# Attention probabilities of a two-layer encoder, transposed by VectorE in 32x32 blocks instead of by TensorE, with the heads in a written order

## The chip, the cores and the metric

The kernel runs on one core of a Trainium2 chip. The metric is the device time of one execution in microseconds. Five engines work beside each other, each through its own queue of instructions: TensorE (PE in the profile; its weight loads are PEld), VectorE (DVE), ScalarE (ACT), GpSimd (POOL) and SyncE (SP), which here issues DMAs.

## The reference, cut to what matters

Two layers; x is 512 x 1024 in float32. In each layer one projection feeds three kinds of attention with heads of 64 features, whose outputs are gated, merged and projected; then comes an MLP.

```python
h = x @ w_in[layer]
qa, ka, va, qb, kb, vb, qc, kc, vc, gate_logits = split(h)
oa = dilated_attention(rot(qa)*scale, rot(ka), va)                 # a: 4 heads, all 512 keys, masked
ob = softmax(axial(rms(qb))*scale @ axial(rms(kb)).T) @ vb         # b: 8 heads, 2 for keys and values
oc = neighbourhood_attention(qc*scale, kc, vc, rpb)                # c: 4 heads, 16-column windows, bias
g = sigmoid(gate_logits + b_gate)
merged = g0*(oa @ w_ba) + g1*(ob @ w_bb) + g2*(oc @ w_bc)
x = LN(alpha*x + merged @ w_out)
x = LN(alpha*x + square(relu(x @ w_up)) @ w_down)
```

## The kernel before, in words

Each float32 factor is held as a pair, hi (rounded) and lo (the rest), and `mm3` (lines 152 to 155) forms a product from three TensorE matmuls: hi hi, hi lo, lo hi. A unit of work below is one such `mm3`.

**Weights** come through `Stream`: SyncE issues a DMA of 512 KB into one of two `raw` buffers, ScalarE copies it to `whi` (line 182), VectorE subtracts to get `wlo` (line 183). A tile holds 8 units of work. Up to 5 split tiles are held, 3 more in a second pool after the heads.

**A layer** projects q and k of a (`a_qk`) and v of a, then goes through 64 blocks: 16 of a, 16 of c, 32 of b. A block is one head times 128 queries. It has two score matmuls (lines 513 and 514; 512 keys in a and b, 256 or 384 in c), the row maximum (line 519 for b, 523 with mask or bias for a and c), its negation (524), the exponential with its row sum (525, ScalarE), the reciprocal of the sum (528), the product with it (529; GpSimd, for c VectorE), and `turn`: TensorE transposes each 128x128 piece into PSUM (line 544, `psp`), and `split_psum` turns that into the pair `pth` (ScalarE, line 228) and `ptl` (VectorE, line 229). After the fourth block of a head, `values` multiplies with v in 8 matmuls; the output is evicted in lines 568 and 569, and for each second head split into `oh` and `ol`.

**Beside the blocks** two lists are served. `Work` holds the other matmuls of the layer (gates, the projections for b and c, the branch products with their results in `psg`, `psq`, `psb`); `pump(rate)` issues so many units twice per block. `Chores` holds small steps: `make_pair` and `prepare` transpose the queries and keys of a pair of heads and split them (lines 446 to 457), `norm_rotate` (lines 368 to 397) normalizes and rotates 128 rows of q and k of b, with a power on GpSimd (380) and sine products on GpSimd (389) between steps on VectorE. `need` (called when a new head begins) finishes whatever its q and k still lack.

**The order** of the instructions on each engine is set by a scheduler, except in the first projection, where the program order is kept. After the heads comes `tail` (gates and branch products of b, merged by line 617 on GpSimd), then the product with `w_out`, LN, the two halves of the MLP, and LN again. All of PSUM's 8 banks are one pool.

## Time and profile before

| | |
|---|---|
| median of 3 runs | 1546.57 us (1546.35 to 1548.46) |
| profiled execution | 1549.4 us, its span 1547.6 us |
| mean granted clock of TensorE | 0.996 |
| heads of layer 1 (46.3 to 302.7 us) | 256.4 us |
| heads of layer 2 (811.6 to 1068.7 us) | 257.1 us |

The span runs from the first to the last recorded instruction; the metric is a little longer. A busy time is the time in which an engine works on at least one instruction; matmuls overlap, so the mean duration of one is longer than the distance between two. Clock 1.00 is 2.4 GHz and 0.50 is 1.2 GHz.

### The profile page before, as it was taken

To read this page: it belongs to the slowest core of one execution; us is meant where nothing else is said; L and a number is where in the kernel's file an instruction comes from. 1 tells how busy PE (TensorE), PEld (TensorE's weight loads), DVE (VectorE), ACT (ScalarE), POOL (GpSimd) and SP (SyncE) were. 2 spreads that over 40 slices of the span, in tenths; PEclk is the share of its full clock that TensorE was granted. 3 is DMA by queue.
4 is the path that set the end of the run, shared out by engine and by line. 5 is a ranking of instruction groups with operands and counts; after the bars stand their busy time and mean duration, and the time that the engine had idled before them with its cause. 6 is when DMAs were issued, how large, how long until landed. Compare 5 with 4: busy or idle time off the path is not lost.

```text
span 1547.6 us, 19148 instructions
## 1 busy us (share of the span) xinstructions
PE 1527.6 (99%) x7400; PEld 1279.8 (83%) x7400; DVE 866.0 (56%) x1498; ACT 632.5 (41%) x1036; POOL 182.0 (12%) x190
## 2 busy tenths in 40 slices
PE   8999999999999999999999999999999999999997
PEld 6888888888898888888888888888888888888886
DVE  4678877644664314441566787776448542244315
ACT  4665666533144212431136556665332431134310
POOL 0113213211100000000102141233111000000001
PEclk9999999999999999999999999999999999999999
DMA  6222311153153323332331323112432432233311
GB/s 218 83 85 75 111 55 58 52 177 123 55 177 96 96 82 96 110 96 83 106 128 56 98 82 103 55 59 95 146 123 83 136 99 92 82 123 95 96 55 55
DMA packets 43434, 150.61 MB, mean 97 GB/s; under 512 B 5072, under 2 KB 5712, under 8 KB 43344
## 3 DMA queue, kind: packets, MB, share of 16 engines
q1 hardware_dynamic: 43344, 149.40, 30.5%
q8 instruction: 58, 0.95, 0.2%
q14 instruction: 32, 0.26, 0.1%
HBM read 145.19 MB, written 4.19 MB: 97 GB/s over the span
## 4 chain that ended last, share of the span: by engine, by line
PE 95%; DVE 2%; ACT 1%; DMA 1%; issue 0%; POOL 0%; SPq 0%; POOLq 0%; DVEq 0%; ACTq 0%
PE psd L155 9%; PE psd L154 9%; PE psd L153 9%; PE psu L154 8%; PE psu L155 8%; PE psu L153 8%; PE psg L155 6%; PE psg L154 6%; PE psg L153 6%; PE psp L544 3%; PE psq L155 2%; PE psq L153 2%; PE psq L154 2%; PE psb L155 2%; PE psb L153 2%; PE psb L154 2%
## 5 line engine op out<-in xcount | busy, mean ns | idle before, releaser
L183 DVE TENSOR_TENSOR wlo<-raw,whi 128x1024 fp32r<-128x1024 f32 (+1 forms) x246 | 306.9, 1248 | 421.5 <-ACT whi L182 420.5
L182 ACT ACTIVATE whi<-raw 128x1024 fp32r<-128x1024 f32 (+1 forms) x246 | 258.4, 1053 | 462.8 <-PE psd L155 143.1
L153 PE MATMUL psu<-xTh,whi 128*128 128x512 f32 (+1 forms) x576 | 210.8, 366 | 0.0
L154 PE MATMUL psu<-xTl,whi 128*128 128x512 f32 (+1 forms) x576 | 210.7, 366 | 0.0
L155 PE MATMUL psu<-xTh,wlo 128*128 128x512 f32 (+1 forms) x576 | 210.5, 365 | 0.0
L153 PE MATMUL psd<-whi,hh 128*128 128x512 f32 x512 | 199.3, 389 | 0.0
L155 PE MATMUL psd<-whi,hl 128*128 128x512 f32 x512 | 199.2, 389 | 0.0
L154 PE MATMUL psd<-wlo,hh 128*128 128x512 f32 x512 | 199.2, 389 | 0.0
L153 PE MATMUL psg<-xTh,whi 128*128 128x512 f32 x384 | 156.8, 408 | 0.0
L154 PE MATMUL psg<-xTl,whi 128*128 128x512 f32 x384 | 151.6, 395 | 0.0
L155 PE MATMUL psg<-xTh,wlo 128*128 128x512 f32 x384 | 151.6, 395 | 0.0
L154 PEld LDWEIGHTS psu<-xTl,whi 128*128 128x128 f32 x576 | 108.6, 189 | 17.7
L153 PEld LDWEIGHTS psu<-xTh,whi 128*128 128x128 f32 x576 | 108.6, 189 | 17.4
L155 PEld LDWEIGHTS psu<-xTh,wlo 128*128 128x128 f32 x576 | 108.6, 189 | 17.4
L266 POOL TENSOR_TENSOR ve<-ve,nhalf 128x1 f32<-128x1 f32 x16 | 24.2, 1513 | 775.0 <-DVE ve L265 775.0
L529 POOL TENSOR_SCALAR p<-p,stat 128x512 f32<-128x512 f32 x96 | 70.7, 737 | 360.2 <-DVE stat L528 242.9
L154 PEld LDWEIGHTS psd<-wlo,hh 128*128 128x128 f32 x512 | 96.1, 188 | 20.0
L153 PEld LDWEIGHTS psd<-whi,hh 128*128 128x128 f32 x512 | 96.1, 188 | 19.9
L155 PEld LDWEIGHTS psd<-whi,hl 128*128 128x128 f32 x512 | 96.1, 188 | 19.8
L153 PE MATMUL psq<-whi,xTh 128*128 128x512 f32 (+1 forms) x256 | 90.0, 351 | 7.2 <-ACT whi L182 6.7
L229 DVE TENSOR_TENSOR ptl<-psp,pth 128x512 fp32r<-128x512 f32 (+2 forms) x128 | 81.6, 637 | 21.2 <-ACT pth L228 19.8
L155 PE MATMUL psq<-whi,xTl 128*128 128x512 f32 (+1 forms) x256 | 87.9, 343 | 0.0
(116 smaller groups left out, 2572.7 us busy)
## 6 DMA issues: line engine op xcount, KB each, us to landing
raw<-in_w_up SPq DMA_DIRECT2D x64, 512.0 KB, 3.6
raw<-in_w_down SPq DMA_DIRECT2D x64, 512.0 KB, 3.5
raw<-in_w_gate SPq DMA_DIRECT2D x48, 512.0 KB, 3.5
raw<-in_w_qkv SPq DMA_DIRECT2D x22, 512.0 KB, 3.6
raw<-in_w_out SPq DMA_DIRECT2D x16, 512.0 KB, 3.6
raw<-in_w_c SPq DMA_DIRECT2D x12, 512.0 KB, 3.5
bias<-in_rpb SPq DMA_DIRECT2D x8, 640.0 KB, 3.9
raw<-in_w_bb SPq DMA_DIRECT2D x8, 512.0 KB, 3.6
```

Of the source, the lines that this page charges most:

```text
L153: nc.tensor.matmul(ps, lhs.hi, rhs.hi, start=start, stop=False)
L154: nc.tensor.matmul(ps, lhs.hi, rhs.lo, start=False, stop=False)
L155: nc.tensor.matmul(ps, lhs.lo, rhs.hi, start=False, stop=stop)
L182: nc.scalar.activation(hi[:, s], raw[:, s], AF.Copy)
L183: nc.vector.tensor_tensor(lo[:, s], raw[:, s], f32(hi[:, s]), op=ALU.subtract)
L229: nc.vector.tensor_tensor(dst.lo, ps, f32(dst.hi), op=ALU.subtract)
L266: nc.gpsimd.tensor_tensor(ve[:, 1:], ve[:, :1], nhalf[:, :1], op=ALU.pow)
L529: (nc.vector if name == "c" else nc.gpsimd).tensor_scalar(p, p, st[:, 3:4], 1.0, op0=ALU.mult, op1=ALU.mult)
L544: nc.tensor.transpose(ps[:, j * P:(j + 1) * P], p[:, j * P:(j + 1) * P], ident)
```

## The change

- `turn` is one VectorE instruction per block, a transpose of the 32x32 blocks of p into `tx` (128 partitions, not yet in their places). `gather` moves the blocks of a head into `ptl` by 16 DMAs of 64 KB from SBUF to SBUF, 4 behind each block of the next head. `settle` makes the pair from it one head later: ScalarE copies `ptl` to `pth`, GpSimd subtracts in place, in 4 pieces. So `values` of a head comes two heads later. The 464 TensorE transposes, their PSUM banks and `split_psum` behind them are gone.
- The maximum comes out negated (line 524 is gone); GpSimd multiplies by the reciprocal in c too.
- Of k, one half is computed, and the other half copied by two DMAs. The preparation of q and k, and the eviction, are chores of smaller steps; the rows of `norm_rotate` go one after another (`rotated`).
- Heads and `tail` are in a written order: each engine's instructions stand as the program emits them. `later` and `catch_up` put off evacuations and weight splits until after a pump. PSUM has three groups of banks: 2 for scores, 3 for q and k, 3 for the rest.
- Split weights: `AHEAD` = 4 in each of two pools; in the heads only the first is used. The raw DMA is issued ahead of a split (`lead`).
- `rate` is new; the gates of c run one ahead of their products; in `tail` two ahead.

```diff
+AHEAD = 4
+FIRST = [1, 1, 0, 0, 0, 0]
+SQ = 32
...
+    GROUPS = {"pss": (0, 2), "psk": (2, 5), "psc": (2, 5), None: (5, 8)}
+    turns = {}
+    ordered = [False]
 
     def bank(name):
-        return psum.tile([P, 512], F32, tag="ps", name=name)
+        group = GROUPS.get(name, GROUPS[None]) if ordered[0] else (0, 8)
+        n = turns.get(group, 0)
+        turns[group] = n + 1
+        return psum.tile([P, 512], F32, tag=f"ps{group[0] + n % (group[1] - group[0])}", name=name)
...
+    soon = []
+
+    def later(f):
+        if ordered[0]:
+            soon.append(f)
+        else:
+            f()
...
+    def catch_up():
+        todo = soon[:]
+        soon.clear()
+        for f in todo:
+            f()
...
-            pool, n = (extra[0], 3) if more else (wts, 5)
+            pool = extra[0] if more else wts
             self.used[more] += 1
-            hi = pool.tile([P, 1024], F32R, tag="whi", name="whi", bufs=n)
-            lo = pool.tile([P, 1024], F32R, tag="wlo", name="wlo", bufs=n)
+            hi = pool.tile([P, 1024], F32R, tag="whi", name="whi", bufs=AHEAD)
...
+            if not self.ready and soon:
+                catch_up()
...
-            self.advance()
+            later(self.advance)
...
+                if tb == TB - 1:
+                    stream.free(w[i])
                 if i == nw - 1:
-                    if tb == TB - 1:
-                        for c in w:
-                            stream.free(c)
-                    evac(tb, ps[tb])
+                    later(lambda tb=tb: evac(tb, ps[tb]))
...
+            while rotated[0] < tb:
+                yield None
...
+            rotated[0] += 1
...
-            own = slice(h * HD, (h + 1) * HD)
-            for i in (h, 1 - h):
-                to = slice(i * HD, (i + 1) * HD)
-                nc.scalar.activation(dst(k.hi[to]), src(ps[own]), AF.Copy)
-                nc.vector.tensor_tensor(dst(k.lo[to]), src(ps[own]), dst(f32(k.hi[own])), op=ALU.subtract)
+            own, other = (slice(i * HD, (i + 1) * HD) for i in (h, 1 - h))
+            nc.scalar.activation(dst(k.hi[own]), src(ps[own]), AF.Copy)
+            yield 1
+            nc.vector.tensor_tensor(dst(k.lo[own]), src(ps[own]), dst(f32(k.hi[own])), op=ALU.subtract)
+            yield 1
+            for t in (k.hi, k.lo):
+                nc.sync.dma_start(f32(t)[other], f32(t)[own])
...
+            def maximum(self):
+                name, h, qb = self.at
+                self.p = pool.tile([P, S], F32, tag="p", name="p", bufs=3)[:, :self.n]
+                self.st = pool.tile([P, LINE], F32, tag="stat", name="stat", bufs=4)
+                if name == "b":
+                    nc.vector.tensor_reduce(self.st[:, 1:2], self.ps, axis=AX.X, op=ALU.max, negate=True)
+                else:
+                    add = (maska[:, (3 - qb) * P:(3 - qb) * P + S] if name == "a"
+                           else bias[h][:, C_OFF[qb]:C_OFF[qb] + self.n])
+                    nc.vector.tensor_tensor_reduce(self.p, self.ps, add, -1.0, 3e38, ALU.add, ALU.min, self.st[:, 1:2])
+
+            def exponential(self):
+                s, sign = (self.ps, 1.0) if self.at[0] == "b" else (self.p, -1.0)
+                nc.scalar.activation(self.p, s, AF.Exp, bias=self.st[:, 1:2], scale=sign, accum_out=self.st[:, 2:3])
+
+            def normalize(self):
+                nc.vector.reciprocal(self.st[:, 3:4], self.st[:, 2:3])
+                nc.gpsimd.tensor_scalar(self.p, self.p, self.st[:, 3:4], 1.0, op0=ALU.mult, op1=ALU.mult)
...
+        def turn(name, h, qb, p):
+
+            if qb == 0:
+                n = len(squares)
+                sq = pool.tile([P, 4, TB, TB, SQ], F32, tag=f"tx{n % 3}", name="tx", bufs=1)
+                squares[name, h] = n, sq
+                for kb in range(TB):
+                    q0, q1 = keys_of(name, kb)
+                    for a, b in ((0, q0), (q1, TB)):
+                        if a < b:
+                            nc.gpsimd.memset(sq[:, :, kb, a:b], 0.0)
...
-            nc.vector.tensor_scalar(st[:, 1:2], st[:, 0:1], -1.0, None, op0=ALU.mult)
-            nc.scalar.activation(p, s, AF.Exp, bias=st[:, 1:2], accum_out=st[:, 2:3])
-
-            def normalize():
-                nc.vector.reciprocal(st[:, 3:4], st[:, 2:3])
-                (nc.vector if name == "c" else nc.gpsimd).tensor_scalar(p, p, st[:, 3:4], 1.0, op0=ALU.mult, op1=ALU.mult)
-
-            return p, normalize
-
-        pts = {}
-
-        def turn(name, h, qb, p):
-            if qb == 0:
-                pts["now"] = Split(pool.tile([P, TB, S], F32R, tag="pth", name="pth", bufs=1),
-                                   pool.tile([P, TB, S], F32R, tag="ptl", name="ptl", bufs=1))
-            pt = pts["now"]
-            k0, k1 = keys_of(name, qb)
-            n = k1 - k0
-            ps = bank("psp")[:, :n * P]
-            for j in range(n):
-                nc.tensor.transpose(ps[:, j * P:(j + 1) * P], p[:, j * P:(j + 1) * P], ident)
-            split_psum(pt[:, k0:k1, qb * P:(qb + 1) * P], ps.rearrange("p (k q) -> p k q", q=P))
+            nc.vector.transpose(squares[name, h][1][:, :, k0:k1, qb].rearrange("p j k b -> p k j b"),
+                                p.rearrange("p (k j a) -> p k j a", j=4, a=SQ))
...
+        def gather(name, h, ms, queues=(nc.sync,)):
+
+            n, sq = squares[name, h]
+            if ms[0] == 0:
+                lo = pool.tile([P, 4, TB, P], F32R, tag=f"ptl{n % 2}", name="ptl", bufs=1)
+                parts[name, h] = Split(None, lo)
+            lo = parts[name, h].lo
+            for m in ms:
+                i, j = m % 4, m // 4
+                queues[m % len(queues)].dma_start(f32(lo)[j * SQ:(j + 1) * SQ, i],
+                                                  sq[i * SQ:(i + 1) * SQ, j].rearrange("a k q b -> a k (q b)"))
...
+        def settle(name, h, kbs, engines=(nc.gpsimd, nc.gpsimd)):
+
+            pt = parts[name, h]
+            if pt.hi is None:
+                pt.hi = pool.tile([P, 4, TB, P], F32R, tag=f"tx{squares[name, h][0] % 3}", name="pth", bufs=1)
+            for kb in kbs:
+                q = keys_of(name, kb)
+                hi, lo = chosen(pt.hi[:, :, kb], *q), chosen(pt.lo[:, :, kb], *q)
+                nc.scalar.activation(hi, f32(lo), AF.Copy)
+                engines[kb % 2].tensor_tensor(lo, f32(lo), f32(hi), op=ALU.subtract)
...
+            chores.add(evict(name, h, po))
+
+        def evict(name, h, po):
+            yield 1
...
-        rate = {"a": 2.1, "c": 2.85, "b": 1.6}
+        rate = {"a": 2.2, "c": 2.5, "b": 1.75}
...
+            for i, (name, h, qb) in enumerate(slots):
+                if i + 1 < len(slots):
+                    todo[i + 1].normalize()
+                score(i + 2)
+                turn(name, h, qb, todo[i].p)
+                if i >= 2 * TB and qb < 3:
+                    settle(*head_of(i - 2 * TB), ((0, 1), (2,), (3,))[qb])
+                catch_up()
+                soften(i + 2)
+                chores.pump()
+                work.pump(rate[name])
+                catch_up()
+                if i >= TB:
+                    gather(*head_of(i - TB), range(4 * qb, 4 * qb + 4))
+                if i >= 2 * TB and qb == 3:
+                    values(*head_of(i - 2 * TB))
+                    if head_of(i - 2 * TB) == ("a", 1):
+                        flags.add("a")
...
+            gather(*head_of(-1), range(16), (nc.sync, nc.scalar))
+            settle(*head_of(-1 - TB), range(TB))
+            while work.queue:
+                work.pump(1)
+                catch_up()
+                chores.pump()
+            ordered[0] = False
...
+            with tc.manual_schedule():
+                values(*a)
+                ts.append(drain(half_gate("b", 0)))
+                settle(*b, range(TB), (nc.vector, nc.gpsimd))
+                ts.append(drain(half_gate("b", 1)))
+                values(*b)
+                chores.flush()
```

**VectorE where the third head of c begins.** `rw` is q and k of b in `norm_rotate` (`cs`, `ss`, `t2` belong to it), `p` and `stat` a block's probabilities and row numbers, `of` an evicted output, `tx` the transposed blocks, `ISA` the masked maximum. Before:

```order
L382 TENSOR_TENSOR rw_698<-rw_698,ss_1482 128x640
L523 ISA p_1452,stat_1453<-pss_1449,bias_1138 128x256
L523 ISA stat_1453 128x1
L524 TENSOR_SCALAR stat_1453<-stat_1453 128x1
L528 RECIPROCAL stat_1453<-stat_1453 128x1
L529 TENSOR_SCALAR p_1452<-p_1452,stat_1453 128x256
L393 TENSOR_TENSOR rw_698<-rw_698,cs_1438 128x512
L229 TENSOR_TENSOR ptl_1430<-psp_1476,pth_1429 128x3x128
L378 TENSOR_REDUCE ss_1557<-sq_1486 128x10
L523 ISA p_1499,stat_1500<-pss_1496,bias_1330 128x256
L523 ISA stat_1500 128x1
L183 TENSOR_TENSOR wlo_1540<-raw_1291,whi_1539 128x1024
```

After:

```order
L427 TENSOR_TENSOR rw_673<-rw_673,cs_1307 128x512
L427 TENSOR_TENSOR rw_673<-rw_673,cs_1307 128x128
L429 TENSOR_TENSOR rw_673<-rw_673,t2_1379 128x640
L662 TENSOR_TENSOR of_1401<-of_1401,pso_1293 64x4x4x32
L409 TENSOR_TENSOR cs_1424<-gqk_296,ropeb_83 128x256
L412 TENSOR_REDUCE ss_1426<-sq_1422 128x10
L413 TENSOR_SCALAR ss_1426<-ss_1426 128x10
L416 TENSOR_TENSOR rw_673<-rw_673,ss_1426 128x640
L427 TENSOR_TENSOR rw_673<-rw_673,cs_1424 128x512
L427 TENSOR_TENSOR rw_673<-rw_673,cs_1424 128x128
L429 TENSOR_TENSOR rw_673<-rw_673,t2_1431 128x640
L598 STREAM_TRANSPOSE tx_1320<-p_1331 128x3x4x32
```

Before, steps of one rotation stand between steps of blocks; after, the last steps of one rotation and all of the next stand together, ahead of the transposes of block `p_1331`.

**VectorE in the heads of b.** `wlo` is the low part of a weight tile, `mg` and `t` gated branch products. Before:

```order
L519 TENSOR_REDUCE stat_2229<-pss_2225 128x1
L607 SCALAR_TENSOR_TENSOR mg_1969<-mg_1969,psb_2221 128x512
L524 TENSOR_SCALAR stat_2229<-stat_2229 128x1
L183 TENSOR_TENSOR wlo_2482<-raw_2334,whi_2481 128x1024
L528 RECIPROCAL stat_2229<-stat_2229 128x1
L519 TENSOR_REDUCE stat_2264<-pss_2260 128x1
L229 TENSOR_TENSOR ptl_2168<-psp_2250,pth_2167 128x4x128
L524 TENSOR_SCALAR stat_2264<-stat_2264 128x1
L528 RECIPROCAL stat_2264<-stat_2264 128x1
L229 TENSOR_TENSOR ptl_2168<-psp_2276,pth_2167 128x4x128
L519 TENSOR_REDUCE stat_2293<-pss_2289 128x1
```

After:

```order
L568 TENSOR_REDUCE stat_2426<-pss_2419 128x1
L579 RECIPROCAL stat_2426<-stat_2426 128x1
L598 STREAM_TRANSPOSE tx_2341<-p_2391 128x4x4x32
L568 TENSOR_REDUCE stat_2449<-pss_2444 128x1
L209 TENSOR_TENSOR wlo_2463<-raw_2385,whi_2462 128x1024
L579 RECIPROCAL stat_2449<-stat_2449 128x1
L598 STREAM_TRANSPOSE tx_2492<-p_2425 128x4x4x32
L706 SCALAR_TENSOR_TENSOR t_2282<-t_2282,psb_2452 128x512
L209 TENSOR_TENSOR wlo_2504<-raw_2460,whi_2503 128x1024
L568 TENSOR_REDUCE stat_2508<-pss_2489 128x1
L662 TENSOR_TENSOR of_2352<-of_2352,pso_2470 64x4x4x32
```

The reciprocal of a block stands behind its own maximum and behind what was emitted since, the transpose of the block before stands behind it, and the next maximum behind that.

**ScalarE in the same place.** `p` is an exponential, `whi` the high part of a weight tile, `pth` that of transposed probabilities, `t` a gate, `qs` queries. Before:

```order
L182 ACTIVATE whi_2481<-raw_2334 128x1024
L525 ACTIVATE p_2228,stat_2229<-pss_2225,stat_2229 128x512
L228 ACTIVATE pth_2167<-psp_2250 128x4x128
L525 ACTIVATE p_2263,stat_2264<-pss_2260,stat_2264 128x512
L228 ACTIVATE pth_2167<-psp_2276 128x4x128
L525 ACTIVATE p_2292,stat_2293<-pss_2289,stat_2293 128x512
L568 ACTIVATE of_2164<-pso_2302 64x512
L228 ACTIVATE pth_2317<-psp_2319 128x4x128
L182 ACTIVATE whi_2574<-raw_2367 128x1024
L228 ACTIVATE oh_2313<-of_2164 128x512
L585 ACTIVATE t_2237<-psg_2244,hb_289 128x512
L228 ACTIVATE pth_2317<-psp_2353 128x4x128
```

After:

```order
L576 ACTIVATE p_2391,stat_2392<-pss_2378,stat_2392 128x512
L491 ACTIVATE qs_2395<-psk_2365 64x512
L491 ACTIVATE qs_2416<-psk_2365 64x512
L625 ACTIVATE pth_2343<-ptl_2219 128x4x128
L576 ACTIVATE p_2425,stat_2426<-pss_2419,stat_2426 128x512
L576 ACTIVATE p_2448,stat_2449<-pss_2444,stat_2449 128x512
L681 ACTIVATE t_2371<-psg_2372,hb_293 128x512
L208 ACTIVATE whi_2462<-raw_2385 128x1024
L625 ACTIVATE pth_2494<-ptl_2360 128x4x128 x2
L208 ACTIVATE whi_2503<-raw_2460 128x1024
L576 ACTIVATE p_2507,stat_2508<-pss_2489,stat_2508 128x512
L659 ACTIVATE of_2352<-pso_2470 64x4x4x32
```

The copy `whi_2462`, on which `wlo_2463` above waits, stands behind the exponential of the same block (`p_2448`) and a gate; before, the copy `whi_2481` for `wlo_2482` stands ahead of the exponential `p_2228`, behind whose maximum that subtraction stands on VectorE.

## Rows read from the trace of the kernel before

**Rows 1.** The page, part 1: busy time, share of the span, instructions of each engine.
```profile
PE 1527.6 (99%) x7400; PEld 1279.8 (83%) x7400; DVE 866.0 (56%) x1498; ACT 632.5 (41%) x1036; POOL 182.0 (12%) x190
```

**Rows 2.** Waits of TensorE: line waited for, us in total, times, longest us.
```profile
PE psp L544 <- POOL p L529: 4.6, 2, 2.3
```

**Rows 3.** Windows: us; busy of PE, PEld, DVE, ACT, POOL; clock; DMA share; GB/s.
```profile
46.30:302.70 256.40, 254.12 (x1299) 212.77 (x1298) 195.62 (x444) 155.54 (x309) 64.66 (x73) 0.99 0.23 72
53.80:57.20 3.40, 3.40 (x9) 2.67 (x8) 1.64 (x5) 1.39 (x3) 0.56 (x1) 0.50 0.38 141
```

**Rows 4.** Lines: the transposes on TensorE; busy us, mean ns, idle before and its releaser.
```profile
L544 PE MATMUL psp<-ident,p 128*128 128x128 f32 x464 | 72.0, 274 | 4.6 <-POOL p L529 4.6
```

**Rows 5.** Timeline of TensorE around four transposes: start us, us, engine, line.
```profile
281.54 0.40 PE L155 MATMUL psg<-xTh,wlo 128*128 128x512 f32 x1
281.77 0.60 PE L544 MATMUL psp<-ident,p 128*128 128x128 f32 x4
...
282.45 0.40 PE L154 MATMUL psg<-xTl,whi 128*128 128x512 f32 x1
```

**Rows 6.** Timeline of all engines at 51.2 us, shortly before the first of the two waits.
```profile
51.25 1.22 DVE L183 TENSOR_TENSOR wlo<-raw,whi 128x1024 fp32r<-128x1024 f32 x1
...
51.32 1.71 POOL L529 TENSOR_SCALAR p<-p,stat 128x512 f32<-128x512 f32 x1 [50.02 <-DVE stat L524]
```

**Rows 7.** Timeline of TensorE: the end of that wait, in brackets the idle time before.
```profile
53.08 0.66 PE L544 MATMUL psp<-ident,p 128*128 128x128 f32 x4 [2.28 <-POOL p L529]
```

**Rows 8.** Line 529: durations ns min/median/max, first and last start.
```profile
L529 POOL TENSOR_SCALAR p<-p,stat x96: 687/696/1711, 51.3 to 1071.3; 128x512 f32<-128x512 f32 x96
```

**Rows 9.** Lines: the other instructions of a block, of weights and evictions.
```profile
L183 DVE TENSOR_TENSOR wlo<-raw,whi 128x1024 fp32r<-128x1024 f32 (+1 forms) x246 | 306.9, 1248 | 421.5 <-ACT whi L182 420.5
L182 ACT ACTIVATE whi<-raw 128x1024 fp32r<-128x1024 f32 (+1 forms) x246 | 258.4, 1053 | 462.8 <-PE psd L155 143.1 <-DMA raw<-in_w_up 88.7 <-PE psu L154 87.6
...
L525 ACT ACTIVATE p<-pss,stat 128x512 f32<-128x512 f32 x64 | 44.0, 687 | 51.1 <-DVE stat L524 50.8
L519 DVE TENSOR_REDUCE stat<-pss 128x1 f32<-128x512 f32 x64 | 43.8, 685 | 3.7 <-PE pss L514 3.3
...
L617 POOL TENSOR_TENSOR mg<-mg,t 128x512 f32<-128x512 f32 x32 | 43.8, 1369 | 158.6 <-DVE t L607 158.6
...
L528 DVE RECIPROCAL stat<-stat 128x1 f32<-128x1 f32 x128 | 20.5, 160 | 44.8 <-ACT p L525 43.9
...
L568 ACT ACTIVATE of<-pso 64x512 f32<-64x512 f32 x32 | 18.9, 591 | 27.3 <-PE pso L559 26.9
...
L525 ACT ACTIVATION_READ_ACCUMULATOR p<-pss,stat 128x1 f32 x64 | 12.4, 194 | 0.0
```

**Rows 10.** Lines by form, VectorE: a PSUM subtraction of 128x512, a query piece of 64x128.
```profile
L229 DVE TENSOR_TENSOR ptl<-psp,pth 128x512 fp32r<-128x512 f32 x96 | 66.1, 689 | 20.4 <-ACT pth L228 19.5
...
L457 DVE SCALAR_TENSOR_TENSOR qs<-psc,qs 64x128 fp32r<-64x128 f32 x32 | 8.5, 286 | 0.7
```

**Rows 11.** Lines: the steps of `norm_rotate`.
```profile
L380 POOL TENSOR_TENSOR ss<-ss,nhalf 128x10 f32<-128x10 f32 x8 | 21.8, 2727 | 57.5 <-DVE ss L379 57.5
...
L389 POOL TENSOR_TENSOR t<-rw,cs 128x256 f32<-128x256 f32 (+1 forms) x32 | 21.0, 686 | 9.1 <-DVE rw L382 3.0 <-DVE stat L524 1.4 <-ACT whi L182 1.4
...
L393 DVE TENSOR_TENSOR rw<-rw,cs 128x512 f32<-128x512 f32 (+1 forms) x16 | 8.4, 525 | 1.6 <-POOL t L389 1.6
...
L382 DVE TENSOR_TENSOR rw<-rw,ss 128x640 f32<-128x640 f32 x8 | 6.6, 823 | 6.7 <-POOL ss L380 6.7
```

**Rows 12.** Timeline of VectorE: two neighbours that do not depend on each other.
```profile
153.76 0.15 DVE L528 RECIPROCAL stat<-stat 128x1 f32<-128x1 f32 x1
153.83 0.53 DVE L229 TENSOR_TENSOR ptl<-psp,pth 128x384 fp32r<-128x384 f32 x1
```

**Rows 13.** DMA issues: count, KB each, median us from issue to landing.
```profile
x_dram<-x SPq DMA_DIRECT2D x8, 256.0 KB, 2.0
...
maska<-in_mask_a SPq DMA_DIRECT2D x2, 448.0 KB, 6.9
```

More of the change, by code (lines that the diff above doesn't have):

```diff
@@ L413, in c_project @@
             got = []
-            yield from wide(got, "psc")
+            yield from wide(got, "psr")
             c_rows[m] = keep.tile([P, S], F32, tag="t", name="ct", bufs=2)
-            nc.scalar.activation(blocks(c_rows[m]), by_columns(got[0]), AF.Copy)
+            later(lambda: nc.scalar.activation(blocks(c_rows[m]), by_columns(got[0]), AF.Copy))
         def c_values(m):
-            while m == 0 and "a" not in flags:
+            while m == 0 and "a" not in flags or m == 1 and ("a", 1) not in oT:
                 yield None
@@ L551, in values @@
                  "c": lambda: V["c", h // 2][:, :, h % 2]}[name]()
-            pt = pts["now"]
+            pt = parts.pop((name, h))
             po = bank("pso")
@@ L682, in need, with score @@
                 chores.flush()
-        probs = deque()
-        def ahead(i):
+        todo = [Block(*x) for x in slots]
+        def score(i):
             if i < len(slots):
-                nxt = slots[i]
-                if nxt[2] == 0:
-                    need(nxt[:2])
-                p, normalize = scores(*nxt)
-                probs.append(p)
-                if nxt[2] == TB - 1:
-                    flags.add(nxt[0] + "abcdefgh"[nxt[1]])
-                return normalize
-            return lambda: None
@@ L720, in attention @@
-        work.flush()
-        stream.plan([a for m in range(KB) for a in g(1, [m]) + ([w_bb[l, m // 2]] if m % 2 == 0 else [])])
-        def tail():
-            steps = 0
-            for m in range(KB):
-                for _ in gated("b", m):
-                    steps += 1
-                    if steps == 4:
-                        values(*slots[-1][:2])
+                if slots[i][2] == 0:
+                    need(slots[i][:2])
+                todo[i].multiply()
+                if slots[i][2] == TB - 1:
+                    flags.add(slots[i][0] + "abcdefgh"[slots[i][1]])
@@ new lines, in soften, with head_of @@
+        def soften(i):
+            if i < len(slots):
+                todo[i].maximum()
+                todo[i].exponential()
+        def head_of(i):
+            return slots[i][:2]
+        stream.lead = True
+        with tc.manual_schedule():
+            ordered[0] = True
+            for i in range(2):
+                score(i)
+                soften(i)
+            todo[0].normalize()
+            for i, (name, h, qb) in enumerate(slots):
[16 more added lines that the diff above has]
+                        flags.add("a")
+                if name == "a" and h == 1 and qb == 0:
+                    chores.add(make_pair("a", 1))
+                if qb == 2 and (name, h) in (("a", 3), ("c", 0), ("c", 1)):
+                    load_bias(1 if name == "a" else h + 2)
+                if "b" in flags and "cc" in flags and "b0" not in flags:
+                    chores.add(make_pair("b", 0))
+                if name == "b" and h % 2 == 1 and h < 7 and qb == 0:
+                    chores.add(make_pair("b", h // 2 + 1))
+                chores.pump()
+                work.pump(rate[name])
+            gather(*head_of(-1), range(16), (nc.sync, nc.scalar))
[3 more added lines that the diff above has]
+                catch_up()
+                chores.pump()
+            ordered[0] = False
@@ L765, in encoder @@
     xp = right.enter_context(tc.tile_pool(name="x", bufs=1, side="right", reuse_waits="tile"))
[L766 removed]
+    extra[0] = right.enter_context(tc.tile_pool(name="early", bufs=1, side="right", reuse_waits="tile"))
+    stream.plan([w_qkv[0, i] for i in range(6)], FIRST)
     def split_x(tb, t, cut):
```

161 lines of the change are left out of this document (96 added, 65 removed).

## The prediction

> **What bounds the kernel now.** Read part 1 of the page first: TensorE is busy 99% of the span, VectorE 56%, GpSimd 12% [rows 1]. So what counts is matmul time and the few moments in which TensorE waits. The heads of layer 1 are the stretch to read next: 256.4 us, TensorE busy 254.1, but VectorE busy 195.6 and ScalarE 155.5 [rows 3]; no other stretch loads VectorE so. TensorE waits for what this change removes in one place only, line 544, twice, 4.6 us together, for the product on GpSimd [rows 2]. After the first of these waits (2.28 us [rows 7]) the granted clock is 0.50 for 3.4 us [rows 3], that is at 1.2 instead of 2.4 GHz: half of the 3.4 us, 1.7, is lost behind each. Last, VectorE's reciprocals: over all blocks it idles 44.8 us ahead of them, 43.9 for the exponential [rows 9]. That wait is harmless as long as other work can be put there.
>
> **What is removed.** 464 transposes leave TensorE [rows 4]. Matmuls overlap, so the cost of one is a distance between starts, not its 274 ns. A 512-column matmul starts 0.23 us after the one before (281.54 to 281.77); from the start of four transposes to the matmul after next 0.68 us pass (281.77 to 282.45) [rows 5], in which one 512-column matmul also stands. Four cost 0.68 - 0.23 = 0.45, so 464 cost 116 x 0.45 = 52.2. With them go the waits, 4.6, and the slow stretches behind them, 2 x 1.7 = 3.4. Gain: 60.2 us. The subtractions to `ptl` on VectorE (0.69 each [rows 10]), the copies to `pth` and the negations lay beside TensorE's work; leaving them out gains nothing by itself.
>
> **What is added, and its price.** The new VectorE transpose stands in no row. The nearest is the 128x512 subtraction out of PSUM, 0.69 us [rows 10]: as many elements written. A weight subtraction, 1.25 for 128x1024 [rows 9], is 0.62 for as many. Below, it could be half of that, 0.31, if elements pass faster with one operand; above, twice the row, 1.38, if the strided order costs two passes. I take 0.69, the row it is nearest to. A GpSimd subtraction in `settle`: between the product with a number, 0.70 [rows 8], and the merge with two operands, 1.37 [rows 9]; I take 1.37, which has the same operands. A gather DMA of 64 KB: between 2.0 us (256 KB) and 6.9 (a mask of 448 KB, with other loads) [rows 13]; I take 2.0. Four of them per block and eight in flight then need 1 us per block; at 6.9 it would be 3.5, about a block's time.
>
> **The loop in b.** In the written order VectorE does for a block: its maximum, then its reciprocal, then the transpose of the block before, then the next maximum. The reciprocal waits for the exponential of the maximum just done. So a block costs VectorE at least 0.685 + 0.687 + 0.194 + 0.160 (maximum, exponential, its sum's readout, reciprocal [rows 9]) + 0.69 = 2.42 us, waiting included, and TensorE cannot run far ahead, since it has two score banks. Into that loop come other steps. For eight blocks, two heads:
> - 8 x 2.42 = 19.3.
> - 28 units of work mean 3.5 weight tiles. Most copies (I count 5 of 6) are put behind the exponential on ScalarE, and the subtraction ahead of the reciprocal on VectorE: 1.05 + 1.25 = 2.30 [rows 9] come on top; for the rest only 1.25. 3.5 x 2.13 = 7.4.
> - Two evictions, copy 0.59 [rows 9] and sum 0.69: 2.6; one split into `oh`, `ol`: 1.3; a pair of queries, 0.59 + 2 x 0.69 = 2.0; a gate and a gated product in the way, 2 x 0.69 = 1.4.
> - Less overlap: an independent neighbour starts 0.07 after a 0.15 us instruction [rows 12], so some 33 VectorE instructions give back 2.3.
>
> Sum 31.7, or 3.96 per block. TensorE needs 3.5 units x 3 + 2 scores + 2 for values = 14.5 matmuls x 0.23 = 3.34. The loop is 0.6 longer; for 32 blocks 19 us. Before, the negation and other blocks' subtractions stood between, and the weight copies earlier, so VectorE filled the wait.
>
> By the same sum a block of a takes 3.95 (2.42, 0.55 tiles x 2.13 = 1.17, evictions 0.32, keys and queries 0.32, less 0.28) against 3.63 (15.8 matmuls): for 14 blocks 4.5, say 5.
>
> **The single waits, per layer.**
> - The third head of c: `need` flushes the chores, all steps of a whole rotation with them. On VectorE, in order: a copy 0.59 and 8 query pieces at 0.286 [rows 10], 2.9; the end of the rotation before, 2 x 0.525 + 0.82 [rows 11], 1.9; a sum 0.7; the next rotation: reduction and two passes over 640 columns at 0.82 (2.5), the small step 0.16, the power on GpSimd 2.73, four sine products 2.74, cosines 1.05 [rows 11], together 9.2. Behind it stand a transpose and a maximum (0.9 for these smaller blocks), the exponential 0.7 to 0.9, and the weight copy 1.05. Sum 17.5, less 14 overlaps of 0.07, is 16.5. TensorE has 20 matmuls left, 4.6. Wait: 12.
> - `bq` takes four tiles 2 units, 1.4 us, apart, while a split takes 2.3: 3 x 0.9 = 2.7, and one block's loop of 2.4 falls between: 5.
> - First c block: two queries, each 0.59 + 4 x 0.286: 3.5.
> - A GpSimd subtraction behind a power, 2.73 + 1.37, and `values` behind it: 4.
> - First pair of b: 0.59 + 0.69, the half of k by DMA 2.0, queries 0.59 + 2 x 0.69: 5.
> - The next-to-last head: settled after the last block, 0.59 + 4 x 1.37 on GpSimd: 6.
>
> These are 35.5, with the loops 19 + 5 = 24 they are 59.5 per layer, 119 for two. Of these waits two per layer are longer than the 2.28 us that had a slow stretch behind it: 4 x 1.7 = 6.8.
>
> **Sum.** 1549.4 (profiled) - 60.2 + 119 + 6.8 = 1615.0. The profiled execution lies 2.8 above the median of 1546.6, so 1612.
>
> **A rule against the change.** The product on GpSimd began 0.07 us behind a weight subtraction and took 1.71 us [rows 6], where the median is 0.70 [rows 8]: it lost 1.0, about what was left of the subtraction. The Trainium skill, "SBUF — State Buffer", section "Who interferes with whom", says that a VectorE instruction with two SBUF inputs and a GpSimd instruction that reads SBUF exclude each other for a whole instruction. By that rule, the trace agrees here, the new GpSimd subtractions would also hold up weight subtractions: GpSimd reads about half of the time in b, a collision costs some 0.35, 0.44 tiles per block, so 0.08 x 128 blocks = 10 us; the sum by it would be 1622.
>
> **The rivals.**
> - The written order holds and the gain arrives. For it: VectorE's total falls (no negations, no product in c), 195.6 of 256.4 leaves room, and even after the cut TensorE's stretch would be some 226. It needs the transpose at the low bound and splits that hide in the wait. Against it: 43.9 us of idle time at the reciprocals already, and a fixed order that can put nothing there by itself. Only the 6 at each tail stay: 1549.4 - 60.2 + 12 - 2.8 = 1498.
> - The loops hide, the single waits come. For it: the rates move work out of c and into b, which evens the load. Against it: 3.96 against 3.34 is not close. 1549.4 - 60.2 + 71 + 6.8 - 2.8 = 1564, slower than before.
> - The transpose costs twice the row, 1.38. 48 blocks of a and b and 16 of c at half: 56 x 0.69 = 39 per layer, 77 in all: 1689. Nothing in the trace excludes it; a VectorE step that reorders is not there. Slow gathers, at the high bound, would end about there too. The Trainium skill, "VectorE: DVE Perf Modes", section "The three transpose paths", gives 311 ns for 128x128 in bf16; an estimate of 4 x 311 = 1.24 us per block, by which the sum would be 1612 + 112 x 0.55 = 1674. No run here shows that yet.
>
> **How the numbers follow.** Forecast 0.54, gain arrives 0.17, single waits alone 0.18, costly transpose 0.11. The forecast's own range: VectorE's loop 0.3 per block either way is 0.3 x 96 = 29, the single waits 40% either way is 28, so 1570 to 1655. The range from 1515 to 1690 leaves out most of the first rival and the tail above the third, together some 0.18. Such a comparison can tell 0.2%, 3 us. Faster by more: the first rival and a little of the second, 0.20; within: 0.03; slower: 0.77.
>
> **What would show it.** In the new profile TensorE's share falls to some 93%; its waits name scores, `psc`, or weight splits; VectorE idles ahead of the reciprocal for the exponential, and ahead of `wlo` for `whi`, in b. One wait above 10 us stands at the third head of c in each layer. The mean of the transpose and of GpSimd's subtraction are there to read. The forecast is wrong if TensorE stays at 99%, if b's blocks come every 3.4 us, or if the transpose is far from 0.69.

## The result, and the profile after

The changed kernel takes 1674.3 us (1668.9 to 1676.8, 4 runs), the kernel before beside it 1547.5 (1546.4 to 1549.1): ratio 1.0814, 95% interval 1.0784 to 1.0844. The forecast was 1612, with a range from 1515 to 1690. The direction came as forecast, and TensorE's share fell to 91% where 93% was forecast; the distance from the kernel before was twice as large, 126.8 us for 65.4.

Part 1 of the page, against [rows 1]:

```profile
PE 1523.8 (91%) x6936; PEld 1256.4 (75%) x6936; DVE 843.3 (50%) x1330; ACT 620.1 (37%) x1024; POOL 354.0 (21%) x378
```

464 matmul instructions are gone, but TensorE's busy time fell by 3.8 us only. Its idle time grew from 1547.6 - 1527.6 = 20.0 to 1671.6 - 1523.8 = 147.8. TensorE's waits (line, us in total, times, longest), against [rows 2]; these are the largest:

```profile
PE pss L560 <- DVE qs L495: 36.8, 13, 4.8
PE psr L178 <- ACT whi L208: 30.9, 2, 15.5
PE psb L178 <- ACT t L681: 11.4, 2, 5.8
PE psq L178 <- ACT whi L208: 10.2, 5, 5.9
...
PE pso L640 <- POOL ptl L626: 8.0, 4, 2.8
```

The first names the queries of a new pair of heads, the second the third head of c (two layers, 15 us each). The wait for GpSimd at line 640 is small. By stages of layer 1 (us; busy time of PE, PEld, DVE, ACT, POOL; clock; DMA share; GB/s; [rows 3] has the heads before as a whole): a, c, b, and the first part of the tail.

```profile
45.30:108.20 62.90, 55.03 (x281) 46.58 (x279) 36.30 (x84) 32.28 (x67) 19.75 (x23) 0.97 0.45 114
108.20:206.10 97.90, 70.59 (x288) 55.04 (x288) 56.90 (x130) 41.31 (x85) 47.78 (x69) 0.86 0.44 118
206.10:346.80 140.70, 117.32 (x472) 92.67 (x473) 84.83 (x142) 71.63 (x142) 63.90 (x66) 0.92 0.45 116
346.80:380.00 33.20, 26.30 (x107) 20.87 (x106) 14.55 (x17) 11.76 (x21) 17.37 (x14) 0.90 0.38 103
```

Idle TensorE: 7.9, 27.3, 23.4 and 6.9 us, 65.5 together. The clock is 0.97, 0.86, 0.92 and 0.90; in the same four stages before it was 0.97, 1.00, 1.00 and 1.00. In the heads and tails of both layers the trace has twenty stretches at clock 0.50, that is at 1.2 GHz, ten per layer. Their sum (us; busy time of each engine; then the means):

```profile
sum 122.89, PE 83.86 PEld 65.38 DVE 74.03 ACT 52.77 POOL 55.11; mean PE 4.19 PEld 3.27 DVE 3.70 ACT 2.64 POOL 2.76
```

TensorE worked 83.9 us at half speed, so 41.9 were lost there. Before there were two such stretches, 6.6 us busy, 3.3 lost.

The two unknown prices by form (busy, mean ns, idle before), against [rows 10] and [rows 9]:

```profile
L626 POOL TENSOR_TENSOR ptl<-ptl,pth 128x512 fp32r<-128x512 f32 x92 | 123.7, 1358 | 31.3 <-ACT pth L625 20.7 <-DMA ptl<-tx 10.6
...
L598 DVE STREAM_TRANSPOSE tx<-p 128x512 f32<-128x512 f32 x96 | 66.8, 696 | 6.4 <-PE pso L640 3.1 <-issue 1.9 <-DMA ptl<-tx 0.9
```

The transpose takes 0.696 us (0.69 was taken from the nearest row), GpSimd's subtraction 1.358 (1.37). Reciprocal and power:

```profile
L579 DVE RECIPROCAL stat<-stat 128x1 f32<-128x1 f32 x128 | 20.3, 159 | 36.8 <-ACT p L576 36.2
...
L414 POOL TENSOR_TENSOR ss<-ss,nhalf 128x10 f32<-128x10 f32 x8 | 15.8, 1972 | 22.7 <-DVE stat L579 17.3 <-DVE ss L413 5.3
```

The reciprocals idle 36.2 us for the exponential, against 43.9 in [rows 9].

### The profile page after: what moved, and what is told of

Same layout as the page of the kernel before. It is cut to its first block, busy times and chain, and to the rows that moved or that the text cites. A ratio compares the mean times of both kernels' runs of the same rounds, so it can differ in the third digit from the quotient of the medians.

```text
span 1671.6 us, 19294 instructions
## 1 busy us (share of the span) xinstructions
PE 1523.8 (91%) x6936; PEld 1256.4 (75%) x6936; DVE 843.3 (50%) x1330; ACT 620.1 (37%) x1024; POOL 354.0 (21%) x378
## 3 DMA queue, kind: packets, MB, share of 16 engines
q1 hardware_dynamic: 70352, 187.18, 38.6%
## 4 chain that ended last, share of the span: by engine, by line
PE 65%; DVE 13%; ACT 9%; issue 5%; DMA 5%; POOL 2%; SPq 1%; ACTq 0%; POOLq 0%; DVEq 0%
PE psu L179 7%; PE psu L178 7%; PE psu L180 7%; PE psd L178 7%; PE psd L179 7%; PE psd L180 7%; ACT whi L208 3%; DVE wlo L209 3%; PE psg L180 3%; PE psg L178 3%; PE psg L179 3%; ACT p L576 3%; PE pso L640 2%; PE psq L179 2%; PE psq L180 2%
## 5 line engine op out<-in xcount | busy, mean ns | idle before, releaser
L209 DVE TENSOR_TENSOR wlo<-raw,whi 128x1024 fp32r<-128x1024 f32 (+1 forms) x246 | 311.3, 1268 | 465.8 <-ACT whi L208 465.7
L580 POOL TENSOR_SCALAR p<-p,stat 128x512 f32<-128x512 f32 (+2 forms) x128 | 86.1, 673 | 349.4 <-DVE stat L579 345.3
L626 POOL TENSOR_TENSOR ptl<-ptl,pth 128x512 fp32r<-128x512 f32 (+2 forms) x124 | 151.5, 1235 | 39.7 <-ACT pth L625 27.3
L178 PEld LDWEIGHTS psg<-xTh,whi 128*128 128x128 f32 x384 | 73.9, 193 | 38.4 <-ACT whi L208 11.0
L178 PE MATMUL psq<-whi,xTh 128*128 128x512 f32 (+1 forms) x256 | 91.4, 357 | 11.6 <-ACT whi L208 10.2
```

The costliest lines, as they stand in the source:

```text
L178: nc.tensor.matmul(ps, lhs.hi, rhs.hi, start=start, stop=False)
L209: nc.vector.tensor_tensor(lo[:, s], raw[:, s], f32(hi[:, s]), op=ALU.subtract)
L580: nc.gpsimd.tensor_scalar(self.p, self.p, self.st[:, 3:4], 1.0, op0=ALU.mult, op1=ALU.mult)
L626: engines[kb % 2].tensor_tensor(lo, f32(lo), f32(hi), op=ALU.subtract)
```

## How the waits come about

The third head of c, timeline of all engines of the changed kernel (start, us, engine, line):

```profile
154.43 0.29 DVE L427 TENSOR_TENSOR rw<-rw,cs 128x128 f32<-128x128 f32 x1 [0.21 <-POOL t L423]
...
155.58 0.68 DVE L662 TENSOR_TENSOR of<-of,pso 64x512 f32<-64x512 f32 x1
...
156.18 0.41 DVE L409 TENSOR_TENSOR cs<-gqk,ropeb 128x256 f32<-128x256 f32 x1
...
157.62 1.98 POOL L414 TENSOR_TENSOR ss<-ss,nhalf 128x10 f32<-128x10 f32 x1 [2.63 <-DVE ss L413]
...
160.54 2.42 POOL L423 TENSOR_TENSOR t<-rw,cs 128x256 f32<-128x256 f32 x4 [0.94 <-DVE rw L416]
...
162.92 1.26 POOL L626 TENSOR_TENSOR ptl<-ptl,pth 128x512 fp32r<-128x512 f32 x1
162.99 1.33 DVE L427 TENSOR_TENSOR rw<-rw,cs 128x128 f32<-128x128 f32 x1 [0.21 <-POOL t L423]
164.36 0.83 DVE L429 TENSOR_TENSOR rw<-rw,t 128x640 f32<-128x640 f32 x1
165.10 0.57 DVE L598 STREAM_TRANSPOSE tx<-p 128x384 f32<-128x384 f32 x1
...
166.23 0.51 ACT L576 ACTIVATE p<-p,stat 128x256 f32<-128x256 f32 x1 [11.93 <-DVE stat L572]
...
170.57 1.99 ACT L208 ACTIVATE whi<-raw 128x1024 fp32r<-128x1024 f32 x2
...
171.66 0.79 PE L178 MATMUL psr<-xTh,whi 128*128 128x512 f32 x1 [15.43 <-ACT whi L208]
```

The rotation begins at 156.18 and ends at 165.2, 9.0 us (forecast: 9.2); only then come the transpose, the maximum, the exponential (its engine idled 11.93) and the weight copy, and TensorE has stood for 15.43 us. Another place, in b:

```profile
230.68 0.16 DVE L579 RECIPROCAL stat<-stat 128x1 f32<-128x1 f32 x1 [0.91 <-ACT p L576]
...
231.27 0.67 ACT L681 ACTIVATE mg<-psg,hb 128x512 f32<-128x512 f32 x1
...
231.84 1.05 ACT L208 ACTIVATE whi<-raw 128x1024 fp32r<-128x1024 f32 x1
...
232.92 1.47 DVE L209 TENSOR_TENSOR wlo<-raw,whi 128x1024 fp32r<-128x1024 f32 x1 [1.13 <-ACT whi L208]
...
234.32 0.68 DVE L568 TENSOR_REDUCE stat<-pss 128x1 f32<-128x512 f32 x1
...
235.09 0.69 ACT L576 ACTIVATE p<-pss,stat 128x512 f32<-128x512 f32 x1 [2.20 <-DVE stat L568]
...
236.43 0.77 DVE L662 TENSOR_TENSOR of<-of,pso 64x256 f32<-64x256 f32 x2 [1.44 <-ACT of L659]
237.11 0.15 DVE L579 RECIPROCAL stat<-stat 128x1 f32<-128x1 f32 x1
...
239.37 0.58 ACT L491 ACTIVATE qs<-psk 64x512 fp32r<-64x512 f32 x1
239.98 0.68 DVE L495 SCALAR_TENSOR_TENSOR qs<-psk,qs 64x512 fp32r<-64x512 f32 x1 [1.38 <-ACT qs L491]
...
240.72 0.79 PE L560 MATMUL pss<-kh,qs 128*128 128x512 f32 x1 [4.80 <-DVE qs L495]
```

On ScalarE the weight copy stands behind a gate; VectorE stands 1.13 us for it, the next maximum comes behind its subtraction and the exponential behind that, then VectorE stands 1.44 for an eviction's copy ahead of the reciprocal, and then for a copy of queries. The score of the next pair has waited 4.80 us. These are the steps of the chain in the forecast, piled up at one place. Scores in b follow here at 2.5, 3.2, 2.5, 6.2, 3.0, 8.2, 4.9, 4.7 us, where the chain was forecast as 3.96 each. Two of these distances hold a wait of TensorE (1.5 in the 6.2, 4.8 in the 8.2), and the 4.9 behind lies in a slow stretch; the rest is TensorE's own work, which is uneven. TensorE's waits in all of b, the largest:

```profile
PE pss L560 <- DVE qs L495: 12.3, 4, 4.8
PE psg L178 <- ACT whi L208: 4.2, 1, 4.2
PE psb L178 <- DVE of L662: 4.2, 1, 4.2
```

Within b's 32 blocks TensorE stands at eight places for 0.5 to 4.8 us, 23.4 together. No line names a block's maximum or exponential: the chain of a block alone does not stop TensorE; what piles up on it at a new pair of heads, a weight copy or an eviction does.

A third place is the tail. ScalarE and TensorE:

```profile
356.79 5.57 ACTq L610 DMA_DIRECT2D ptl<-tx  x8
362.53 2.19 ACT L625 ACTIVATE pth<-ptl 128x512 fp32r<-128x512 f32 x4 [11.52 <-DMA ptl<-tx]
...
365.35 0.79 PE L178 MATMUL psb<-oh,whi 128*128 128x512 f32 x1 [5.83 <-ACT t L681]
```

ScalarE's queue issues eight of the last head's gather DMAs over 5.6 us, then come four copies to `pth`, which had to wait, and only behind them the gate `t` for which TensorE has stood 5.83 us. The path through DMAs costs time here, by ScalarE's queue and not by GpSimd.

Behind a wait the clock falls; one for queries in b and the stretch behind it:

```profile
276.20:279.40 3.20, 0.02 (x1) 0.02 (x1) 1.76 (x4) 1.29 (x4) 0.00 (x0) 1.00 0.70 149
280.20:283.60 3.40, 3.40 (x10) 2.67 (x9) 2.43 (x5) 1.19 (x3) 1.75 (x3) 0.53 0.24 56
```

3.2 us idle, then 3.4 at clock 0.53. Of the ten slow stretches of layer 1, where two were forecast, eight stand behind a single wait of 2.9 us or more and two behind several of 0.3 to 1.7 us.

## The experiments

Theory A: the written order makes TensorE wait, through what stands ahead of reciprocals, scores and weight splits on VectorE and ScalarE. Theory B, also called C or the path theory: the new path itself (transposes, 16 DMAs a head, GpSimd's subtractions) is too slow in any order. Theory D: the other edits cost. Medians of 4 runs; the ratio to the kernel before with its interval.

**Order and transposes, a table of two by two.**

```diff
-        with tc.manual_schedule():
+        with nullcontext():
```

This is the edit in the heads; the tail has it twice more.

> The changed kernel, but heads and tail are ordered by the scheduler again, as in the kernel before; transposes on VectorE, gather DMAs, settle, PSUM groups and rates stay. Theory A (TensorE's waits come from the written order: what stands ahead of a reciprocal, a score or a weight split on VectorE and ScalarE): the 45 us of idle and slow clock per layer in the heads go, 1674 falls to 1500 to 1540. Theory B (the new path itself is too slow, transposes, 16 DMAs a head and the subtractions on GpSimd, whatever the order): it stays above 1620.

Measured: 1659.9 (1.0729, 1.0703 to 1.0755). Theory A's number failed, B's came. Waits of VectorE in this run:

```profile
DVE tx L598 <- POOL ptl L626: 53.8, 11, 6.3
...
DVE tx L598 <- POOL p L580: 31.6, 40, 3.7
```

The transposes stand for GpSimd: 53.8 us for the subtraction whose operand lies in the buffer that they write next, and 31.6 for the product. So under the scheduler it is the path that holds up VectorE; how much of the time that is, the edits of the subtraction below show.

```diff
-    GROUPS = {"pss": (0, 2), "psk": (2, 5), "psc": (2, 5), None: (5, 8)}
+    GROUPS = {"pss": (0, 2), "psp": (0, 2), "psk": (2, 5), "psc": (2, 5), None: (5, 8)}
...
+            pt = parts[name, h]
+            ps = bank("psp")[:, :n * P]
+            for j in range(n):
+                nc.tensor.transpose(ps[:, j * P:(j + 1) * P], p[:, j * P:(j + 1) * P], ident)
+            split_psum(pt[:, k0:k1, qb * P:(qb + 1) * P], ps.rearrange("p (k q) -> p k q", q=P))
```

> The changed kernel with its written order, but with the transposes on TensorE and the split out of PSUM by ScalarE and VectorE, as before; no gathers and no settling; values one head later; the banks of the transposes are taken from the two of the scores. Theory A (the written order makes the waits): 52 us of matmul work come on top, some of it in waits, VectorE's chain keeps 0.69 per block for the subtraction: 1660 to 1720. Rival C (the path of VectorE, DMAs and GpSimd is what costs): 1550 to 1600.

Measured: 1745.9 (1.1288, 1.1269 to 1.1307). The written order without the new path is the slowest of all. Part of that may be the experiment's own: the score banks are shared with the transposes, and waits of scores appear that the changed kernel does not have (TensorE's waits):

```profile
PE pss L560 <- DVE qs L495: 31.0, 12, 3.7
PE pss L560 <- ACT p L576: 29.3, 27, 2.5
PE pss L560 <- DVE stat L572: 22.1, 8, 9.5
```

The last two are 51.4 us, against 0.4 in the changed kernel. Without them it would still be some 20 us above the changed kernel; the clock behind these waits is not in this sum. The fourth cell:

> The fourth cell of a table of two by two: all other edits of the change kept (rates, groups of banks, 4 split buffers, chores, values one head later), but transposes on TensorE as before and the order by the scheduler. Written order with VectorE 1674, with TensorE 1746, scheduler with VectorE 1660. Theory A (the written order costs, the other edits little): 1550 to 1590, and then the new path costs some 80 under the scheduler. Theory D (the other edits, above all the three groups of banks and what is put off until after a pump, cost by themselves, whatever the order): 1640 to 1740.

Measured: 1564.3 (1.0100, 1.0084 to 1.0115), with both edits above. TensorE hardly waits there:

```profile
PE pss L560 <- DVE stat L572: 7.4, 8, 2.0
PE psq L178 <- ACT whi L208: 6.8, 1, 6.8
```

| | transposes on TensorE | on VectorE |
|---|---|---|
| order by the scheduler | 1564.3 | 1659.9 |
| written order | 1745.9 | 1674.3 |

Theory D is out under the scheduler, where its edits cost 16 us; in the written order they were not taken out one by one. The written order costs 182 us with TensorE's transposes; up to 51 of them, and the slow clock behind, may be due to the shared banks. (They are shared in the scheduler's cell too, where scores wait 7.4 us.) The path on VectorE costs 96 under the scheduler, although TensorE's transposes are gone with it, and gives back 72 in the written order. The two costs do not add; the next two runs show for one step of the path that its waits lie under those of the order.

**The subtraction on GpSimd, in both orders.**

```diff
-                engines[kb % 2].tensor_tensor(lo, f32(lo), f32(hi), op=ALU.subtract)
```

> The scheduler's order with VectorE transposes, and GpSimd's subtraction in settle left out (so the low part of the probabilities is the whole again and the output is not the reference's). In that order VectorE's transposes wait 54 us for this subtraction, since its operand lies in the buffer of the next transposes. Path theory: 25 to 60 us come back from 1660. Theory D: the wait moves to the next step of the path or to banks, less than 15.

Measured: 1595.6 (1.0301, 1.0284 to 1.0318), 64 us less.

> The changed kernel in its written order, GpSimd's subtraction in settle left out (the output is not the reference's). Under the scheduler this gave back 64 us. Theory A (in the written order VectorE's and ScalarE's queues set the waits; the changed kernel's TensorE waits only 8 us for this subtraction): 5 to 20 us come back with slow stretches, 1674 falls to 1654 to 1669. Path theory (the path sets the end in both orders): 40 to 70 us come back, 1605 to 1635.

Measured: 1659.1 (1.0716, 1.0698 to 1.0733), 15 us less. So two thirds of what the path costs under the scheduler is this subtraction, and in the written order it is hidden but for 15: for this step theory A holds in the changed kernel, and the path theory in the scheduler's order. The edit takes away GpSimd's time as well as the hold on the buffer; which of the two counts is not separated.

**The chain of a block.**

```diff
-            nc.vector.transpose(squares[name, h][1][:, :, k0:k1, qb].rearrange("p j k b -> p k j b"),
-                                p.rearrange("p (k j a) -> p k j a", j=4, a=SQ))
+            for _ in range(2):
+                nc.vector.transpose(squares[name, h][1][:, :, k0:k1, qb].rearrange("p j k b -> p k j b"),
+                                    p.rearrange("p (k j a) -> p k j a", j=4, a=SQ))
```

> The changed kernel, each VectorE transpose is issued twice. Theory A with a loop (VectorE's chain of maximum, exponential, reciprocal and transpose sets the pace of most blocks): 0.70 us x 96 and 0.50 x 32 blocks are 83 us, of which more than half shows: 1674 rises by 45 to 90. Rival (most blocks run at TensorE's pace, and the loss is in single long waits): it rises by less than 30.

Measured: 1724.3 (1.1137, 1.1120 to 1.1154), 50 us for 82.7 of added work, theory A's number. TensorE's idle time grew from 147.8 to 180.2. So the chain matters, although in the changed kernel it stops TensorE only where other steps pile up on it.

```diff
-                turn(name, h, qb, todo[i].p)
...
                 soften(i + 2)
+                turn(name, h, qb, todo[i].p)
```

> The changed kernel, but the transpose of a block is put behind the next but one block's maximum on VectorE instead of ahead of it, so that it runs while the exponential is taken for which the next reciprocal waits. Theory A (the chain maximum, exponential, reciprocal, transpose sets the pace where VectorE is behind): 0.7 us per block leave the chain; as doubling the transpose cost 50 us, 35 to 60 come back, 1674 falls to 1615 to 1640. Rival C (the long single waits and the path through DMAs and GpSimd set the time, so that every order ends near the scheduler's 1660): less than 15 us.

Measured: 1648.1 (1.0655, 1.0628 to 1.0683), 26 us less: between the two expectations. The reciprocal's line in this run:

```profile
L579 DVE RECIPROCAL stat<-stat 128x1 f32<-128x1 f32 x128 | 21.0, 164 | 12.8 <-ACT p L576 11.8
```

Its wait for the exponential fell from 36.2 to 11.8, 24.4 us, about what was gained. The chain is there; that the other transposes had no such wait to fill fits with the number, but was not tested.

**Single waits.**

```diff
-                chores.flush()
+                if key[0] == "c":
+                    chores.prepare_until(lambda: (key[0], key[1] // 2) in pairs)
+                else:
+                    chores.flush()
```

> The changed kernel, but at the first and third head of c only the steps that make their own q and k are finished; the steps of the rotation for b stay in the list. Theory A: the 24 us between two scores at the third head of c fall to about 6, and with the idle time half of a slow stretch goes: 18 per layer, 1674 falls to 1630 to 1645. Rival (the rotation has to be done on VectorE anyway and now delays other blocks or the first pair of b): less than 10 us come back, 1664 to 1676.

Measured: 1660.8 (1.0727, 1.0711 to 1.0743), 13.5 us less, neither theory's number. TensorE's waits show where the rest went:

```profile
PE psk L485 <- DVE rw L443: 13.3, 2, 6.7
...
PE pso L654 <- ACT pth L639: 12.4, 2, 6.2
...
PE psr L192 <- ACT whi L222: 11.4, 2, 5.7
```

The wait at the projection fell from 30.9 to 11.4; 13.3 us came up where b's first pair needs the rotated rows, 12.4 where values need the copy `pth`.

```diff
                 work.pump(rate[name])
-                catch_up()
                 if i >= TB:
```

> The changed kernel, but evacuations and weight splits are caught up once per block, ahead of the maximum, and no longer between an exponential and its reciprocal. Theory A: a copy of weights no longer stands behind the exponential that the reciprocal waits for; up to 1.05 us per tile for some 50 tiles, and slow stretches with them: 1674 falls by 20 to 60. Rival (TensorE then gets its weights and banks half a block later and waits for them instead): no change or slower, 1674 to 1700.

Measured: 1678.6 (1.0843, 1.0827 to 1.0859): no gain, as the rival said. Copy and subtraction moved together, and evacuations with them. TensorE's idle time is 147.7 us, where it was 147.8: its branch products wait less for evictions (3.5 us for 8.7), and it waits more for `mg` (9.2 for 0.2), so one wait was exchanged for others.

> Two edits together: the transpose behind the maximum, and no rotation flushed at the third head of c (which alone gave 13.5 us). Theory A: the two are about additive, 1600 to 1630. Rival C: no faster than 1650.

Measured: 1636.8 (1.0577, 1.0561 to 1.0593), 37.5 less; singly they gave 26.2 and 13.5. Nearly additive; the number is a little above what was expected. On top of these two, only the low parts put off:

```diff
-                nc.vector.tensor_tensor(lo[:, s], raw[:, s], f32(hi[:, s]), op=ALU.subtract)
...
+                self.lows.append(w)
...
                 catch_up()
+                stream.catch_low()
                 soften(i + 2)
```

> The transpose behind the maximum, no rotation flushed (1637 together), and the low part of a weight tile on VectorE is put off to the next block's begin, behind the reciprocal, so that VectorE does not stand waiting for the copy behind an exponential. Theory A: about half of 60 tiles per layer pair stood so, 1.05 us each, a third to a half of it shows: 1637 falls to 1600 to 1625. Rival: TensorE waits for the low parts or for banks instead, 1632 to 1645.

Measured: 1622.1 (1.0473, 1.0457 to 1.0489), 14.7 less, in theory A's range. Unlike the edit that moved all together, this one separates the subtraction from the copy it waits for. It is the fastest written order here; none beats the kernel before.

**The clock.**

```diff
+        def keep_busy(ps, n):
+            k = ps.shape[-1] // P
+            for _ in range(n):
+                nc.tensor.matmul(ps, xT.hi[:, 0, 0], xT.hi[:, :k, 0], start=True, stop=True)
...
+            if name == "psr" and c_rows:
+                keep_busy(ps, 60)
...
+                if qb == 0 and h % 2 == 0 and (name, h) != ("a", 0):
+                    keep_busy(self.ps, 12)
```

> The changed kernel with extra matmuls whose results are overwritten: 12 ahead of the first score of each pair of heads but the first (2.8 us), 60 (13.8 us) ahead of the projection that waits at the third head of c, where TensorE sits idle for 3 to 5 and 15 us. If the slow clock behind waits is part of the loss (theory A's clock term), some 1.7 to 3 us come back at each of some 8 places per layer, since TensorE stays busy: 1674 falls by 10 to 40, and the mean clock rises. Rival (VectorE's and ScalarE's queues set the end, TensorE's clock doesn't matter there): no change or slower by what was added outside of waits, 1674 to 1700.

Measured: 1664.7 (1.0767, 1.0749 to 1.0785), 10 us less with 288 matmuls more. Part 1 of the page, and the clock (0.962 in the changed kernel):

```profile
PE 1571.1 (95%) x7224; PEld 1298.1 (78%) x7224; DVE 841.6 (51%) x1330; ACT 620.0 (37%) x1024; POOL 354.6 (21%) x378
```

```profile
core 0: 1661.5 us, clock 0.978
```

Of the 288, 240 have 512 columns and 48 have 256; at 0.23 us [rows 5] and half of that they are 61 us. The busy time rose by 47.3 only, so some 13 us of slow work were given back. The stretches at clock 0.50 say the same: TensorE is busy in them for 54.9 us, 27.5 lost, where 41.9 were lost in the changed kernel. Idle time fell from 147.8 to 90.4, about what the added work fills. Work that nobody needs made the kernel faster: the slow clock is part of the loss.

## Why the prediction came out as it did

- **The sum, term by term.** Forecast were -52.2 for the transposes, +3.4 for the clock (6.8 - 3.4) and +114.4 for idle time (119 - 4.6), 65.6 together. The profiled execution shows +38.6 for the clock (41.9 - 3.3) and +127.8 for idle time. TensorE's busy time fell by 3.8, so without the slow stretches it fell by 42.4. Together +124.0: the clock is 35.2 of the 58.4 that the forecast lacks, idle time 13.4, the smaller gain 9.8.
- **The gain, 52.2 us.** The instructions are gone as counted. That 42.4 shows instead is worked out from busy times and not measured on the transposes; which instructions took the 9.8 more stays open. In b the slow stretches cost 10.2 of the 117.3 us of busy time, so TensorE's work per block at the full clock is 107.1 / 32 = 3.35 us, where 3.34 was forecast.
- **The new prices.** 0.696 for 0.69 and 1.358 for 1.37 are right. A gather DMA took 2.7 us to landing for 2.0, and that it holds up ScalarE was not in the forecast: the copies to `pth` of 128x512 idle 34.6 us for it, and the wait at the tail is of this kind.
- **The waits, 59.5 per layer.** Idle in layer 1 is 65.5. By stages, forecast first: a with the first block of c 5 + 3.5 = 8.5 and 7.9; c with the first pair of b 12 + 5 + 4 + 5 = 26 and 27.3; b 19 and 23.4; tail 6 and 6.9. The third head of c (15.4 for 12) and the first block of c (2.9 for 3.5) came by their mechanism. The tail did not: 6 was forecast for subtractions on GpSimd, and 5.8 of the 6.9 is the gate behind ScalarE's gathers. That this number fits is luck. In a, the 5 of the loop came as four waits for weights, queries and values, 4.9 together.
- **The evenness of b was wrong.** I spread the chain over all blocks. It comes in lumps, where weight copy, eviction and queries meet in one block.
- **The step that failed** is "Of these waits two per layer are longer than the 2.28 us that had a slow stretch behind it: 4 x 1.7 = 6.8". There are ten slow stretches per layer in the heads and the tail, and they cost 41.9 us. The list above that sentence has itself five waits of 3.5 us or more per layer besides the one at `bq`, so two was too few on its own terms; and the lumps of b, which were spread, make further ones.
- **The rule on the shared port.** In the timeline of the third head of c, GpSimd's subtraction began at 162.92, the VectorE product of 128x128 at 162.99; it took 1.33 us, where such a one took 0.29 at 154.43. This is what the Trainium skill, "SBUF — State Buffer", section "Who interferes with whom", says of VectorE with two inputs in SBUF beside a GpSimd instruction that reads SBUF; the trace agrees. On VectorE's side it was small as a whole: the weight subtractions take 1.268 us on average, 1.248 in [rows 9], 5 us for all 246.
- **The page's price.** The Trainium skill, "VectorE: DVE Perf Modes", section "The three transpose paths", gives 311 ns for 128x128 in bf16; an estimate for four is 1.24 us. Here 128x512 in float32 takes 0.696; the measurement decides. The sum by that price was 1674, which is the measured time, by luck: a transpose cost little more than half of 1.24, and the time went elsewhere.
- **The rivals.** That the gain arrives is refuted: each version that computes all is at least 4.7% above before with the new path. That the loops hide is half right: in b TensorE waits at eight places and nowhere else. The rival with a transpose at twice the row, 1689, came nearer to the time than the forecast and is wrong by its mechanism, 0.696 and not 1.38.
- **Left open:** what the 16 us of the other edits under the scheduler are; how much of 1745.9 is due to shared score banks, and how much of the changed kernel's time to the other edits in the written order; a written order that brings the queries of a pair earlier was not tried.

## What to carry to other kernels

Where every queue is in order, sum an engine's chain with its waits, and then look where the rare steps (weight copies, evictions, the next pair's queries) meet in one block: here the mean came near to the idle time, and the lumps decided how often the clock fell. An operation taken off the bounding engine must be priced by its buffers too: under the scheduler the new path cost 96 us, 64 of them for one subtraction, whose operand lies in a buffer that the next transposes need. Test order and operation in a table of two by two; here each alone would have given the wrong cause.

## What the runs showed of the hardware that was not expected

- Extra matmuls of no use shortened the kernel by 10 us, since they filled idle time and fewer stretches ran at 1.2 GHz (54.9 us of busy time for 83.9).
- The power on GpSimd took 1.97 us in the changed kernel and 2.73 in [rows 11], with the same operands. In the two runs with TensorE's transposes, whose instructions differ in order alone, it took 1.97 (written) and 2.42 (scheduler); the cause stays open.
